# Convolution kernel: two input loads asked for one block earlier

## The chip, the cores and the metric

The kernel runs on one core of a Trainium2 chip. The metric is the device time of one execution in microseconds (us), lower is better. Before the change three runs took 125.30, 125.17 and 125.36 us, median 125.3.

## The reference

The kernel computes a 3 x 3 convolution with padding 1 over 16 images of 64 channels and 64 x 64 pixels, into 128 output channels, all float32 in memory. Nine tenths of the weights are zero, without a pattern that the kernel uses.

```python
batch, c_in, h, w, c_out, k = 16, 64, 64, 64, 128, 3
x_pad = np.pad(x, ((0, 0), (0, 0), (pad, pad), (pad, pad)), mode='constant')
for b in range(batch):
    for co in range(c_out):
        for ci in range(c_in):
            for kh in range(k):
                for kw in range(k):
                    if weight[co, ci, kh, kw] != 0:
                        output[b, co] += weight[co, ci, kh, kw] * x_pad[b, ci, kh:kh+h, kw:kw+w]
```

## The kernel before

**Tiling.** Two images form a pair: 2 x 64 channels fill the 128 partitions. There are eight pairs, 0 to 7, and each is cut into four blocks of 16 output rows, so there are 32 blocks in all, numbered k = 0 to 31; pair p has the blocks 4p to 4p + 3. For a block three inputs are prepared in bfloat16: `sums` (each even row plus the odd row below it), `odd` (the odd rows) and `even` (the even rows). TensorE multiplies them with transformed weights into PSUM, in the order sums, odd, even. One product is shared by the two output rows of a couple; ScalarE copies it from PSUM to `pc`, and VectorE adds it to each of the other two products, writing the even and the odd output rows into a pair's output buffer.

**Who does what.** GpSimd issues all loads of x except the first half of pair 0, and makes `sums` and `even` for the blocks 1 to 31 (lines 287 to 299). ScalarE makes `odd` and `pc` (lines 302 to 307). VectorE does the two additions (lines 310 to 324). SyncE loads the weights and pair 0's first half, and issues the stores (lines 327 to 338, the last one at line 384). TensorE runs a loop of two blocks a turn (lines 368 to 378). Each engine takes its instructions in order, and semaphores tie them together.

**GpSimd's order.** It runs ahead of TensorE by at most two blocks: before it fills `sums` or `even` for block k, it waits until TensorE has finished the product that reads the same buffer for block k - 2. After the fills of block k it issues the load that the table `WHEN` names for k, if there is one:

```python
    PIECES[4] = [(0, 16), (16, H)]
    WHEN = {1: (4, 0), 6: (4, 1), 8: (5, 0), 13: (6, 0)}
...
        for fill_in, product in ((fill_sums, 2), (fill_even, 6)):
            if k >= UNROLL:
                wait(g, s_pe, 6 * (k - UNROLL) + product)
            fill_in(k)
        if k in WHEN:
            load(*WHEN[k])
```

An entry (p, i) is part i of pair p. Pairs 0 (its second half) to 3 are asked for at the start. Pair 4, the fifth, comes in two parts: rows 0 to 15 behind block 1, rows 16 to 63 behind block 6. Pair 5, the sixth, comes whole behind block 8, pair 6 behind block 13, and pair 7 in pieces behind the blocks 18 and 19 (`GROUPS`).

**Loads and buffers.** A load reads float32 from memory and writes bfloat16 into SBUF; only pair 0's first half stays float32. The pairs 0 to 2 lie in the buffer `home`, which becomes an output buffer later; the pairs 3 to 6 have buffers of their own (`x3` to `x6`), so no load of them waits for a buffer. All loads that GpSimd issues go through one DMA queue, q0 in the profile.

**Stores.** SyncE issues the store of pair p once its four blocks are complete: 4 MB a pair, in halves for the pairs 6 and 7. They go through q1. Output buffers are four, taken in turn: `o0`, `o1`, `o2` and `home`; before VectorE writes pair p >= 4 it waits for the store of pair p - 4 (line 315). Loads and stores share the same 16 DMA engines.

Of the kernel before, what the change touches and what calls it, by code (L numbers as in the profile page):

```python
# [22 lines left out]
def kernel(  # L23
# [15 lines left out]
    PIECES = {p: [(0, H)] for p in range(NP)}  # L39
    PIECES[0] = [(HEAD, H)]  # L40
    PIECES[4] = [(0, 16), (16, H)]
    WHEN = {1: (4, 0), 6: (4, 1), 8: (5, 0), 13: (6, 0)}

# [65 lines left out]
    def load(p, i=0):  # L111
        a, b = PIECES[p][i]
        nc.gpsimd.dma_start(out=xs[p][:, a:b, :], in_=pair(p)[:, a:b, :]).then_inc(s_x[p][i], 16)
# [176 lines left out]
    for k in range(1, N):  # L290
# [6 lines that stand above are left out]
        for group in GROUPS.get(k, ()):  # L297
# [124 lines left out]
```

## Time and profile before

| What | us |
|---|---|
| Median of the three runs | 125.30 |
| Profiled execution, its own time | 125.27 |
| Its span, first to last instruction | 123.4 |
| TensorE's first product of block 0 | 7.73 |
| Last addition on VectorE ends | 112.92 |
| Last store issued | 113.21 |
| TensorE busy | 110.1 |
| VectorE busy | 82.6 |
| GpSimd busy | 65.7 |
| ScalarE busy | 54.6 |

The span is the time from the first instruction to the last one. The profiled execution's own time is 1.9 us more than its span, and agrees with the median. Issuing a DMA takes an engine 0.4 to 0.6 us and is not counted as busy time; the transfer itself runs on the 16 DMA engines, and is seen in the rows of the queues: packets, megabytes, and the time of the packets as a share of 16 engines' time in the window. Packets overlap a little, so a full window shows a share slightly over 100%. Bytes are counted where they are written, so that a load from float32 into bfloat16 counts half of what it reads. The issues of the loads and stores that the text speaks of, with the time from issue to landing:

| Transfer | issued at, us | KB written | to landing, us |
|---|---|---|---|
| Pair 4, rows 0 to 15 | 9.31 | 256 | 15.5 |
| Store of pair 0 | 22.17 | 4096 | 16.2 |
| Pair 4, rows 16 to 63 | 24.80 | 768 | 13.8 |
| Pair 5 | 31.28 | 1024 | 16.8 |
| Store of pair 1 | 35.14 | 4096 | 20.2 |
| Pair 6 | 47.49 | 1024 | 15.0 |

### The profile page before, as it was taken

The page shows a single profiled execution, that of the slowest core. Times are in us where ns is not written, and L with a number is a line of the kernel's source. Part 1 is how long each engine was busy: PE and PEld are TensorE (multiplying, and loading weights), DVE is VectorE, ACT ScalarE, POOL GpSimd, SP SyncE. Part 2 cuts the span into 40 slices and gives each one's busy share as a digit, 9 for nine tenths or more (in the row PEclk, how much of TensorE's full clock was granted, in tenths as well). Part 3 has the DMA queues.
Part 4 walks back from the last instruction along what each step waited for, and adds up shares of the span by engine and source line. Part 5 has one row for each costly group of instructions (what it writes and reads, how often), then busy time and mean ns, then how long its engine had stood idle before and what let it go on. Part 6 is the DMA issues. An engine that isn't in the chain of part 4 may idle for free.

```text
span 123.4 us, 2490 instructions
## 1 busy us (share of the span) xinstructions
PE 110.1 (89%) x983; PEld 56.8 (46%) x983; DVE 82.6 (67%) x74; ACT 54.6 (44%) x79; POOL 65.7 (53%) x92
## 2 busy tenths in 40 slices
PE   5999999999999999999999999999999999991000
PEld 1435555555555555555555555555555555550000
DVE  0577777777777777777777777777777777776000
ACT  4544444555555555544444444445555555530000
POOL 4579555575755557555559975555555565200000
PEclk9999999999999999999999999999999999999755
DMA  4999999999999999999999999999999999999993
GB/s 125 350 220 215 215 215 218 274 436 380 324 311 244 321 316 420 388 297 340 345 425 433 357 341 357 408 345 404 424 428 425 425 428 417 428 422 428 428 428 167
DMA packets 4643, 42.79 MB, mean 347 GB/s; under 512 B 538, under 2 KB 538, under 8 KB 1312
## 3 DMA queue, kind: packets, MB, share of 16 engines
q1 hardware_dynamic: 3008, 34.90, 67.5%
q0 software_dynamic: 1632, 7.87, 31.3%
q14 instruction: 3, 0.02, 0.0%
HBM read 17.07 MB, written 33.55 MB: 410 GB/s over the span
## 4 chain that ended last, share of the span: by engine, by line
PE 83%; DVE 2%; issue 0%; DVEq 0%
PE ps L350 83%; DVE home L322 1%; DVE home L318 1%; DVEq L170 0%
## 5 line engine op out<-in xcount | busy, mean ns | idle before, releaser
L305 ACT COPY pc<-ps 128x1024 f32<-128x1024 f32 x32 | 32.4, 1012 | 51.8 <-PE ps L350 51.8
L350 PE MATMUL ps<-even,wT 64*128 64x504 bf16 (+1 forms) x384 | 47.3, 377 | 0.0
L350 PE MATMUL ps<-odd,wT 64*128 64x504 bf16 (+1 forms) x384 | 47.3, 377 | 0.0
L318 DVE TENSOR_TENSOR o<-ps,pc 128x1024 f32<-128x1024 f32 x24 | 29.4, 1225 | 19.6 <-PE ps L350 19.6
L350 PEld LDWEIGHTS ps<-even,wT 64*128 64x128 bf16 x384 | 21.8, 94 | 19.7
L350 PEld LDWEIGHTS ps<-odd,wT 64*128 64x128 bf16 x384 | 21.8, 94 | 19.7
L322 DVE TENSOR_TENSOR o<-ps,pc 128x1024 f32<-128x1024 f32 x24 | 29.4, 1225 | 0.0
L350 PE MATMUL ps<-sums,wT 64*128 64x504 bf16 (+1 forms) x192 | 26.5, 377 | 0.1
L207 POOL TENSOR_TENSOR sums<-x 128x512 bf16<-128x512 bf16 x16 | 18.5, 1156 | 0.1
L196 POOL COPY even<-x 128x576 bf16<-128x576 bf16 (+1 forms) x16 | 10.4, 651 | 14.6 <-PE ps L350 14.6
L350 PEld LDWEIGHTS ps<-sums,wT 64*128 64x128 bf16 x192 | 10.8, 94 | 10.2 <-issue 0.6
L207 POOL TENSOR_TENSOR sums<-home 128x512 bf16<-128x512 bf16 (+1 forms) x11 | 13.3, 1213 | 2.2 <-DMA home<-in_x_dram 2.1
L318 DVE TENSOR_TENSOR home<-ps,pc 128x1024 f32<-128x1024 f32 x8 | 9.8, 1225 | 6.3 <-PE ps L350 6.3
L196 POOL COPY even<-home 128x576 bf16<-128x576 bf16 (+2 forms) x11 | 6.7, 610 | 8.2 <-PE ps L350 8.0
L187 ACT COPY odd<-x 128x576 bf16<-128x576 bf16 (+1 forms) x16 | 10.6, 661 | 0.0
L322 DVE TENSOR_TENSOR home<-ps,pc 128x1024 f32<-128x1024 f32 x8 | 9.8, 1225 | 0.0
L187 ACT COPY odd<-home 128x576 bf16<-128x576 bf16 (+1 forms) x10 | 6.6, 658 | 0.0
L263 PE MATMUL ps<-idle_rhs 128*128 128x512 bf16 x14 | 5.2, 537 | 1.4 <-DVE idle_rhs L228 1.4
L197 POOL MEMSET even<- 128x64 bf16 x8 | 1.2, 154 | 9.4 <-PE ps L350 9.4
L196 POOL COPY even<-x_last 128x576 bf16<-128x576 bf16 (+2 forms) x5 | 2.7, 557 | 4.2 <-PE ps L350 4.2
L207 POOL TENSOR_TENSOR sums<-x_last 128x512 bf16<-128x512 bf16 x4 | 4.6, 1153 | 0.0
L263 PEld LDWEIGHTS ps<-idle_rhs 128*128 128x128 bf16 x14 | 1.7, 130 | 3.7 <-issue 1.9
(26 smaller groups left out, 25.6 us busy)
## 6 DMA issues: line engine op xcount, KB each, us to landing
out_dram<-o SPq DMA_DIRECT2D x5, 4096.0 KB, 19.2
out_dram<-home SPq DMA_DIRECT2D x1, 4096.0 KB, 21.1
out_dram<-o SPq DMA_DIRECT2D x2, 2048.0 KB, 13.6
out_dram<-home SPq DMA_DIRECT2D x2, 2048.0 KB, 10.3
x<-in_x_dram POOLq DMA_DIRECT2D x3, 1024.0 KB, 16.8
home<-in_x_dram POOLq DMA_DIRECT2D x2, 1024.0 KB, 12.8
home<-in_x_dram SPq DMA_DIRECT2D x1, 1024.0 KB, 5.5
x<-in_x_dram POOLq DMA_DIRECT2D x1, 768.0 KB, 13.8
```

The lines of the kernel that those rows point to most:

```text
L187: copy or (lambda o, i: nc.scalar.copy(out=o, in_=i)),
L196: copy or (lambda o, i: nc.gpsimd.tensor_copy(out=o, in_=i)),
L197: zero or (lambda o: nc.gpsimd.memset(o, 0.0)),
L207: engine.tensor_tensor(out=sums[k % UNROLL], in0=src[:, q0 : q0 + ROWS : 2, :], in1=src[:, q0 + 1 : q0 + ROWS : 2, :], op=ADD,).then_inc(s ...
L263: t.matmul(idle_ps, idle_rhs[:, 0:128], idle_rhs, start=True, stop=True)
L305: a.copy(out=pc[k % 3], in_=ps[0]).then_inc(s_pc, 1)
L318: v.tensor_tensor(out=o[:, :, r0 : r0 + ROWS : 2, :], in0=ps[1], in1=pc[k % 3], op=ADD).then_inc(s_free, 1)
L322: v.tensor_tensor(out=o[:, :, r0 + 1 : r0 + ROWS : 2, :], in0=ps[2 + k % 2], in1=pc[k % 3], op=ADD).then_inc(s_out, 1)
L350: mm = t.matmul(into[:, n, :, c_lo:c_hi], tap(g, kw, n), src[q, i : i + HALF, c_lo + kw - 1 : c_hi + kw - 1], start=(m == 0), stop=(m == l ...
```

## The change

One line differs. The second part of pair 4 is asked for behind block 5 in place of block 6, and pair 5 behind block 7 in place of block 8. On GpSimd's queue each of the two load instructions moves up past one `sums` addition and one `even` copy; the other engines' instructions and their order are the same.

```diff
     PIECES[4] = [(0, 16), (16, H)]
-    WHEN = {1: (4, 0), 6: (4, 1), 8: (5, 0), 13: (6, 0)}
+    WHEN = {1: (4, 0), 5: (4, 1), 7: (5, 0), 13: (6, 0)}
```

## The prediction

> **What bounds the kernel now.** I read the page's head and slices first, then the chain of waits, then the DMA queues in chosen windows, and last GpSimd's timeline around the two places. The chain ends with VectorE's last addition (start, length, what):
>
> ```profile
> 7.73 102.64 PE ps L350 x948
> ...
> 111.69 1.23 DVE home L322
> ```
>
> So TensorE runs from 7.73 to 110.37 with nothing between, and the result is complete at 112.92. But the span is 123.4 us, so 10.5 us lie behind the last arithmetic. They belong to the last store, issued at 113.21 (SyncE's timeline):
>
> ```profile
> 113.21 0.37 SPq L384 DMA_DIRECT2D out_dram<-home  x1
> ```
>
> In a window around that issue, time from issue to landing:
>
> ```profile
> out_dram<-home SPq DMA_DIRECT2D x1, 2048.0 KB, 9.4
> ```
>
> 9.4 us for 2.10 MB is too long for the transfer alone. The queue's price comes from a stretch with stores only, 92 to 101 us (queue: packets, MB, share of 16 engines):
>
> ```profile
> q1 hardware_dynamic: 251, 3.88, 101.0%
> ```
>
> 9.0 us for 3.88 MB is 2.32 us per MB, so the last store needs 2.10 x 2.32 = 4.9 us; the other 4.5 us it stood behind earlier stores and the start of a transfer. The slices of the page say since when there is a backlog:
>
> ```profile
> DMA  4999999999999999999999999999999999999993
> GB/s 125 350 220 215 215 215 218 274 436 380 324 311 244 321 316 420 388 297 340 345 425 433 357 341 357 408 345 404 424 428 425 425 428 417 428 422 428 428 428 167
> ```
>
> The 16 DMA engines are full from the second slice to the last but one. Bytes are counted as written; a load reads four bytes for each two it writes, which is why the second to seventh slices show half the rate and are full all the same. Loads only, 8 to 22 us:
>
> ```profile
> q0 software_dynamic: 418, 3.03, 103.7%
> ```
>
> 14.0 us for 3.03 MB is 4.62 us per MB written. With both prices the whole program can be added up: section 3 of the page gives 34.90 MB on q1 and 7.87 MB on q0, so 34.90 x 2.32 + 7.87 x 4.62 = 81.0 + 36.4 = 117.4 us, against about 120 us of busy DMA (from 2 to 122). The kernel is bound by DMA work. What can move its end is the DMA time lost or won, not when a load is asked for.
>
> **The change, GpSimd's side.** No instruction is added or removed. Two load issues move up one block, each past one sums addition and one even copy on GpSimd's queue. GpSimd's timeline of before:
>
> ```profile
> 20.95 0.66 POOL L196 COPY even<-home 128x576 bf16<-128x576 bf16 x1 [1.43 <-PE ps L350]
> 21.62 1.15 POOL L207 TENSOR_TENSOR sums<-home 128x512 bf16<-128x512 bf16 x1
> 24.19 0.66 POOL L196 COPY even<-home 128x576 bf16<-128x576 bf16 x1 [1.43 <-PE ps L350]
> 24.80 0.57 POOL L113 DMA_DIRECT2D x<-in_x_dram  x1
> 25.39 1.16 POOL L207 TENSOR_TENSOR sums<-home 128x512 bf16<-128x512 bf16 x1
> ...
> 28.10 1.16 POOL L207 TENSOR_TENSOR sums<-home 128x512 bf16<-128x512 bf16 x1
> 30.68 0.66 POOL L196 COPY even<-home 128x576 bf16<-128x576 bf16 x1 [1.42 <-PE ps L350]
> 31.28 0.57 POOL L113 DMA_DIRECT2D x<-in_x_dram  x1
> ```
>
> The copy at 20.95 is block 5's even. The first issue goes behind it, to about 21.6. Block 6's sums then run 22.2 to 23.35 in place of 21.6 to 22.8; the copy behind them waits for TensorE until 24.19 anyway, and TensorE takes block 6's sums at 27.17 (its timeline). So 0.57 us is hidden in a wait of 1.43, with 3.8 us left before TensorE would notice. Block 7's sums come 0.54 earlier. The second issue goes from 31.28 to about 28.1; block 8's sums then run 28.7 to 29.8, the copy behind them waits until 30.68, TensorE takes them at 33.66. Cost: 0. If the cover were gone, 2 x 0.57 = 1.1 us of TensorE delay would still lie before the last store's issue at 113.21, which could come some 2.6 us later without emptying the DMA queues (the packets end at about 122.2, so the last store has its turn from 122.2 - 4.9 = 117.3; less about 1.5 us from issue to first byte, as store 0 shows, issued at 22.17 and with no packet in the window to 23.6 and its first in the next). SyncE's queue has the same instructions in the same order.
>
> **The change, who gains from an earlier landing.** Nobody. In the table of waits the only wait for data of x on GpSimd is 2.1 us at the start, on ScalarE 0.4. The second part of pair 4 lands at 24.80 + 13.8 = 38.6 and is first read with block 16, whose even copy needs row 16 at 56.6 (GpSimd's timeline); pair 5 lands at 31.28 + 16.8 = 48.1 and is used from block 20, whose sums come some 19 us later. Worth of 3.2 us earlier: 0.
>
> **The change, the DMA engines.** The loads are 768 and 1024 KB, 0.79 + 1.05 = 1.84 MB, 8.5 us of DMA time at 4.62. Store 0 (issued 22.17) and store 1 (35.14) are 4.19 MB each, 9.7 us. Before, stores ran alone from 24.6 to 28.6 (q1 at 101.4%, no q0), then loads and stores mixed. Now the loads stand behind pair 4's first part, whose last bytes move at about 24.4, and mix with store 0 from its start. Work until 47 is the same either way: store 0 and both loads are done by 24.4 + 9.7 + 8.5 = 42.6, store 1 runs alone behind them. Store 0 lands near 42.6, not 22.17 + 16.2 = 38.4; its buffer is overwritten from block 16, at 61.9 on VectorE, 19 us later. Gain from the order alone: 0, because no engine was empty that now gets work.
>
> One thing is not 0: the price of mixing. Where load 6 mixes with stores, 52 to 61 us, it costs nothing:
>
> ```profile
> q0 software_dynamic: 126, 1.03, 54.6%
> q1 hardware_dynamic: 127, 1.82, 48.3%
> ```
>
> 1.03 x 4.62 + 1.82 x 2.32 = 8.98 us in 9.0. But where the two moved loads run, 28.6 to 42 us:
>
> ```profile
> q1 hardware_dynamic: 188, 2.82, 52.3%
> q0 software_dynamic: 211, 1.34, 50.6%
> ```
>
> 2.82 x 2.32 + 1.34 x 4.62 = 12.73 us in 13.4: **0.67 us of DMA time is lost there**, 0.38 of it from 28.6 to 36.6, 0.23 from 36.6 to 39 and the rest to 42 (same arithmetic). The trace doesn't show why. After the change these loads meet other packets of the stores. Bounds: the loss goes, -0.67; or it spreads over the whole stretch with loads, 24.4 to 42.6, at its worst local rate (0.23 of 2.4, 9.6%): 1.75, so +1.1. At the mean rate of 5% it is 0.91, so +0.24. I take 0, the nearest row being that very stretch with the same loads and the same store.
>
> From 36.6 to 39 q0 has 102.3% and q1 2.8% though store 1 was issued at 35.14: a fresh store starts some 4 us late when a load is under way. The Trainium skill, DMA: Bandwidth & Descriptors, section Queues, rings and completion order, has each engine go round the queues with work after each packet. By that rule the change only swaps turns, and the sum is 0 as well; this row departs from strict turns for 2.4 us, so the rule is no proof that the 0.67 stays.
>
> **Sum.** 0 (GpSimd) + 0 (landings) + 0 (order) + 0 (loss kept, -0.67 to +1.1). The profiled run took 125.27 us (123.4 span and 1.9 around it); the median is 125.30. Forecast 125.3. A measurement of this kernel tells 0.2%, 0.25 us, from no change.
>
> **Rivals.**
> (B) The loss goes, as it is absent where load 6 mixes. For it: of the mixed stretches with large packets this alone loses 5%; the loads now follow one another and end together with store 0, so the start of mixing at 28.6 and the load-only stretch from 36.6 to 39 vanish, where 0.61 of the 0.67 sits or begins. Against: the loss could belong to these addresses, which don't change. Time 125.27 - 0.67 = 124.6 in full, 124.9 for half.
> (C) Slower: the loss grows, because store 0 now shares the engines through its whole length. The place is 24.4 to 42.6 us; the price 5% to 9.6% of 18.2 us against 0.67 now, +0.24 to +1.1, so 125.5 to 126.4, middle 125.8; it decides once the mixed stretch loses over 0.92 us (0.67 + 0.25). For it: the mixing stretch in which a loss is seen gets longer. Against: 52 to 61 mixes as densely at no loss.
> (D) The change does not do what it says at the engines: load bytes don't move earlier, since before there were some 4 us from the issue at 24.80 to first bytes. Then nothing changes, 125.3. Against: here q0 is still working when the request comes, so it follows on.
>
> **From cases to numbers.** Forecast (own range 125.0 to 125.55) 0.34, B 0.32, C 0.30, D 0.04. Range: from nearly all of B (124.5, a little below the full 124.6 for run scatter) to most of C (126.0), leaving out about 0.1 to 0.2. Faster by over 0.2%: B and 0.04 of the forecast's edge, 0.36. Slower: C and 0.03 of the edge, 0.33. Within: 0.31.
>
> **What would show it.** Right: q0 busy without a break from about 24 to 43 in the DMA windows; store 0 landing near 42.6; TensorE's chain still 7.73 to 110.4; the same bytes on both queues; at 52 to 61 us the same rows as before. Which case it is shows in the lost time of 24 to 47 by the two prices: 0.69 us now (1.85 MB and 5.93 MB in 23.0), near 0 for B, over 0.95 for C. Wrong altogether: TensorE idle before block 6 or 8, a different end of the chain, or the last store's 9.4 us changed by something later than 52 us.

## The result and the profile after

The changed kernel is slower. In the first comparison its median is 126.10 us against 125.17 for the kernel before (22 runs each), a ratio of 1.0069 with a 95% interval of 1.0047 to 1.0090. Two later comparisons of the same kernel gave 1.0023 (1.0004 to 1.0042) and 1.0028 (1.0001 to 1.0055). So it costs 0.2 to 0.7%. Medians are those of all executions, ratios and intervals those of the undisturbed ones, so the two can differ slightly. Its profiled execution took 126.35 us with a span of 124.5; before, 125.27 and 123.4.

Arithmetic has not moved. The chain of waits of the changed kernel (start, length, what):

```profile
7.76 102.64 PE ps L350 x948
...
111.73 1.22 DVE home L322
```

TensorE runs the same 102.64 us and VectorE ends at 112.95, before 112.92. On GpSimd the two loads stand where the change puts them:

```profile
20.99 0.66 POOL L196 COPY even<-home 128x576 bf16<-128x576 bf16 x1 [1.42 <-PE ps L350]
21.59 0.57 POOL L113 DMA_DIRECT2D x<-in_x_dram  x1
22.18 1.16 POOL L207 TENSOR_TENSOR sums<-home 128x512 bf16<-128x512 bf16 x1
24.23 0.66 POOL L196 COPY even<-home 128x576 bf16<-128x576 bf16 x1 [0.88 <-PE ps L350]
...
28.11 0.57 POOL L113 DMA_DIRECT2D x<-in_x_dram  x1
```

The wait before block 6's even copy shrinks from 1.43 to 0.88 us, about the 0.57 of the issue, and the copy starts on time. The loss is in the transfers. The slices of the changed kernel:

```profile
DMA  3999999999999999999999999999999999999992
GB/s 121 349 222 216 219 216 213 175 222 338 346 332 321 361 434 437 374 303 308 384 421 397 376 340 390 378 351 433 405 428 426 442 416 416 429 426 424 434 429 95
```

The engines look as full as before. The place shows in the rates: the eighth and ninth slices (21.8 to 28.0 us) move 175 and 222 GB/s, before 274 and 436. The rows of the queues from 23.4 to 28 us (queue: packets, MB, share of 16 engines) in the changed kernel:

```profile
q0 software_dynamic: 157, 0.58, 84.8%
q1 hardware_dynamic: 21, 0.34, 17.8%
```

And in the kernel before:

```profile
q1 hardware_dynamic: 110, 1.80, 91.8%
q0 software_dynamic: 80, 0.13, 15.5%
```

Shares come to over 100% in both. By the prices of the prediction (2.32 us per MB stored, 4.62 per MB loaded) the changed kernel did 0.34 x 2.32 + 0.58 x 4.62 = 3.47 us of work in 4.6 us and lost 1.13; the kernel before lost nothing. A packet that is in flight counts as busy however slowly it goes, so the share alone doesn't show this loss. The bytes do, and so does the time of one packet: from 25 to 26.5 us the changed kernel moves 33 load packets of 6 KB at a share of 98.6%, which is 0.986 x 16 x 1.5 / 33 = 0.72 us each. In the kernel before, from 30 to 33 us, 46 such packets at 45.3% take 0.453 x 16 x 3 / 46 = 0.47 us each. So the loss is packets that take half as long again, not engines that stand empty.

A part of this window shows who moves and who doesn't. From 23.4 to 26.6 us in the changed kernel:

```profile
q0 software_dynamic: 140, 0.48, 105.4%
q1 hardware_dynamic: 3, 0.05, 3.7%
```

Which store stands there? Store 0 was issued at 22.21 and its row says how long it took; the last store's row shows what is left of the loss at the end:

```profile
out_dram<-o SPq DMA_DIRECT2D x1, 4096.0 KB, 23.4
...
out_dram<-home SPq DMA_DIRECT2D x1, 2048.0 KB, 10.4
```

Store 0 lands after 23.4 us in place of 16.2, the last store after 10.4 in place of 9.4. How much of the last store is still to begin at 121.5 us, in the window from there to 126, first in the kernel before:

```profile
q1 hardware_dynamic: 16, 0.04, 2.3%
```

and then in the changed kernel:

```profile
q1 hardware_dynamic: 47, 0.25, 13.5%
```

0.21 MB more, at 2.32 us per MB: the engines are 0.49 us behind on average. From 24 to 47 us (5.75 MB on q1, 1.84 MB on q0) the changed kernel loses 23.0 - 5.75 x 2.32 - 1.84 x 4.62 = 1.16 us, 0.47 more than the 0.69 of before. The loss that the kernel before has from 28.6 to 42 us, 0.67, is gone; the changed kernel's rows there give 13.4 - 3.15 x 2.32 - 1.32 x 4.62 = -0.01 us:

```profile
q1 hardware_dynamic: 192, 3.15, 55.8%
q0 software_dynamic: 190, 1.32, 47.1%
```

The span grew by 1.1. The remainder is put down to unevenness: before, no packet starts after 122.5; in the changed kernel six do, and one of them after 123.0, so some engines end later than the mean. The rows don't tell the 16 engines apart.

### The profile page after: what moved, and what is told of

Read it like the earlier page. It is cut to its first block, busy times and chain, and to the rows that moved or that the text cites. A ratio compares the mean times of both kernels' runs of the same rounds, so it can differ in the third digit from the quotient of the medians.

```text
span 124.5 us, 2490 instructions
## 1 busy us (share of the span) xinstructions
PE 109.9 (88%) x983; PEld 57.3 (46%) x983; DVE 82.6 (66%) x74; ACT 54.6 (44%) x79; POOL 65.7 (53%) x92
## 4 chain that ended last, share of the span: by engine, by line
PE 82%; DVE 2%; issue 0%; DVEq 0%
PE ps L350 82%; DVE home L318 1%; DVE home L322 1%; DVEq L170 0%
## 5 line engine op out<-in xcount | busy, mean ns | idle before, releaser
L350 PE MATMUL ps<-sums,wT 64*128 64x504 bf16 (+1 forms) x192 | 26.5, 377 | 0.4 <-PEq L361 0.4
L207 POOL TENSOR_TENSOR sums<-x 128x512 bf16<-128x512 bf16 x16 | 18.5, 1155 | 0.1
L196 POOL COPY even<-x 128x576 bf16<-128x576 bf16 (+1 forms) x16 | 10.4, 650 | 14.6 <-PE ps L350 14.6
L350 PEld LDWEIGHTS ps<-sums,wT 64*128 64x128 bf16 x192 | 10.9, 94 | 10.4 <-issue 0.8
## 6 DMA issues: line engine op xcount, KB each, us to landing
out_dram<-home SPq DMA_DIRECT2D x1, 4096.0 KB, 23.4
x<-in_x_dram POOLq DMA_DIRECT2D x1, 768.0 KB, 13.4
```

Of the source, the lines that this page charges most:

```text
L196: copy or (lambda o, i: nc.gpsimd.tensor_copy(out=o, in_=i)),
L207: engine.tensor_tensor(out=sums[k % UNROLL], in0=src[:, q0 : q0 + ROWS : 2, :], in1=src[:, q0 + 1 : q0 + ROWS : 2, :], op=ADD,).then_inc(s ...
L350: mm = t.matmul(into[:, n, :, c_lo:c_hi], tap(g, kw, n), src[q, i : i + HALF, c_lo + kw - 1 : c_hi + kw - 1], start=(m == 0), stop=(m == l ...
```

## The experiments

Below, "lost from 16 to 62 us" is 46 us less the work done in them by the two prices. The window takes in all that the versions move; packets over its edges make it uncertain by one or two tenths. It is 1.11 us for the kernel before and 1.50 for the change.

**e1: only the second part of pair 4 moves.**

```diff
-    WHEN = {1: (4, 0), 6: (4, 1), 8: (5, 0), 13: (6, 0)}
+    WHEN = {1: (4, 0), 5: (4, 1), 8: (5, 0), 13: (6, 0)}
```

> Only the second part of pair 4 moves (behind block 5); pair 5 stays behind block 8. In the profile of the changed kernel the DMA engines lose most of their extra time from 23.4 to 26.6 us, where that part moves alone right behind the first part and store 0, issued at 22.2, has not begun: 0.48 MB x 4.62 + 0.05 MB x 2.32 = 2.35 us of work in 3.2. Theory (that part's early request is the cost): slower than before by 0.5 to 1.0 us, about the same as the full change, and the same loss of some 0.85 us between 23.4 and 26.6. Rival (pair 5 behind it, so that store 0 shares the engines through its whole length): no change, within 0.25 us.

Measured: 125.85 us against 125.50, ratio 1.0015 (0.9992 to 1.0038). The theory's 0.5 to 1.0 us is missed: 0.15% is 0.2 us, which the rival allows, and the time alone leaves the question open. Its rows from 23.4 to 28 us don't:

```profile
q0 software_dynamic: 174, 0.68, 101.6%
q1 hardware_dynamic: 4, 0.07, 3.4%
```

0.68 x 4.62 + 0.07 x 2.32 = 3.30 us of work in 4.6: 1.30 lost, as with the full change, with pair 5 still behind block 8. From 16 to 62 us it loses 1.96. The profiled execution took 126.22, above its own median, so these sizes are those of a run worse than the usual one. In it the store was issued at 23.07 and the load 0.62 us ahead, as in the change.

**e2: only pair 5 moves.**

```diff
-    WHEN = {1: (4, 0), 6: (4, 1), 8: (5, 0), 13: (6, 0)}
+    WHEN = {1: (4, 0), 6: (4, 1), 7: (5, 0), 13: (6, 0)}
```

> Only pair 5 moves (behind block 7); the second part of pair 4 stays behind block 6. Theory (the cost is the other request): within 0.25 us of before, and the window 23.4 to 26.6 with stores at over 90% as before. Rival (pair 5 is the cost): slower by 0.5 to 1.0 us.

Measured: 125.48 against 125.50, ratio 0.9991 (0.9968 to 1.0014). Lost from 16 to 62 us: 1.04; nothing from 23.4 to 28. Pair 5's request is free, and the loss hangs on pair 4's second part. It also repeats the kernel before's own loss: 0.64 us from 28.6 to 42, before 0.67.

**e3: the second part a block earlier still.**

```diff
-    WHEN = {1: (4, 0), 5: (4, 1), 7: (5, 0), 13: (6, 0)}
+    WHEN = {1: (4, 0), 4: (4, 1), 7: (5, 0), 13: (6, 0)}
```

> The second part of pair 4 is asked for behind block 4 (about 18.4 us), a block earlier still, with pair 5 behind block 7. Its packets still move from about 24 us, but its request is then 5 us old and not under 2. If the loss comes from a request that is too fresh when its turn comes, it goes: within 0.3 us of before. If it comes from that part's packets meeting the start of store 0 (issued at 22.2 in both), it stays: slower by 0.5 to 1.0 us, with some 0.85 us lost from 23.4 to 26.6.

Measured: 126.26 against 125.50, ratio 1.0042 (1.0020 to 1.0065). A request that is 5 us old costs as well, so its freshness isn't the cause. The profiled execution took 127.64, far above the median, and its rows are not read.

**e4: pair 4 in one load.**

```diff
-    PIECES[4] = [(0, 16), (16, H)]
-    WHEN = {1: (4, 0), 5: (4, 1), 7: (5, 0), 13: (6, 0)}
+    PIECES[4] = [(0, H)]
+    WHEN = {1: (4, 0), 7: (5, 0), 13: (6, 0)}
```

> Pair 4 is asked for in one load behind block 1, and pair 5 behind block 7. Same bytes; rows of 64 x 64 in one piece, and no packets of 2 KB and 6 KB written. If any load that moves alone while store 0 starts loses time, this is slower than before by 0.5 to 1.0 us with the loss again between 23.4 and 27 us. If the loss belongs to the cut in two (two loads over the same rows of memory, packets of 6 KB), it is within 0.3 us of before or faster.

Measured: 125.50 against 125.50, ratio 0.9996 (0.9977 to 1.0016). By its time this speaks for the cut as the cause, by its profile against: from 23.4 to 28 us it loses 4.6 - 0.66 x 4.62 - 0.33 x 2.32 = 0.79 us with no cut and no packets of 6 KB. It saves something elsewhere: the small packets of the first part are dear. In the kernel before, from 22.2 to 23.6, q0 wrote 0.25 MB in 1.4 us, 0.24 us more than the price of large ones. From 16 to 62 us the lost time is 1.32 against 1.11; those 0.2 us are within its interval. So the loss in the rows doesn't need the cut; that it costs time without the cut isn't shown.

**e5 and e9: the change, measured twice more.**

> The changed kernel once more, beside the others of this group on one chip. Theory so far: a store that is freshly issued while loads keep the DMA engines busy makes the load packets in front of it slow until its own first packets move; the change lets pair 4's second part run on exactly when store 0 is issued (22.2 us), where the kernel before had only the last packets of the small first part. Expected: slower by 0.3 to 0.9%, with 0.8 to 1.4 us lost from 23.4 to 28 us and the last packets of the span 0.5 us or more apart from the first engine's last. A rival would be that the 0.7% belongs to one chip: then within 0.2%.

> The changed kernel a third time, since its two intervals so far are 1.0047 to 1.0090 and 1.0004 to 1.0042 times the kernel before. Theory: between 0.2 and 0.7% slower, with about 1 us lost between 23.4 and 28 us. Rival (chance on one chip): within 0.2%.

Measured: 125.94 against 125.57, ratio 1.0023 (1.0004 to 1.0042), and 125.90 against 125.56, ratio 1.0028 (1.0001 to 1.0055). Lost from 23.4 to 28 us: 0.90 and 0.88. The loss is there each time and smaller than the 1.13 of the first profile. The 0.23% of e5 lies below its expected 0.3 to 0.9%; e9 lies within its own. The unevenness is smaller too: in neither does a packet start after 123.0.

**e6: store 0 in two halves, loads as before.** The first half is then issued at 15.88, beside loads of whole pairs that nobody moved.

```diff
-    HALVED = (6, 7)
+    HALVED = (0, 6, 7)
...
-            wait(v, s_st[p - 4][0], 16)
+            for landed in s_st[p - 4]:
+                wait(v, landed, 16)
```

> The table of loads as before; pair 0's store goes out in two halves, so that the first is issued behind block 1, at about 15.7 us, beside loads of whole pairs. Theory (a fresh store beside running loads): 0.5 us or more lost in 16 to 21 us, where the kernel before loses nothing (loads alone, 4.62 us per MB); the time is slower by 0.2 to 0.8 us unless losses at 28.6 to 42 go. Rival (the loss belongs to pair 4's or pair 5's rows in memory): nothing lost in 16 to 21 us, within 0.25 us of before.

Measured: 125.57 against 125.57, ratio 0.9996 (0.9979 to 1.0014). The rows from 16 to 22 us:

```profile
q0 software_dynamic: 143, 1.04, 90.4%
q1 hardware_dynamic: 32, 0.26, 10.7%
```

And in the kernel before, where loads run alone in this window:

```profile
q0 software_dynamic: 175, 1.30, 103.9%
```

1.04 x 4.62 + 0.26 x 2.32 = 5.41 us of work in 6.0: 0.59 lost, before -0.01. With the store's issue 6.3 us earlier, a loss appears among loads of other pairs and other addresses. No byte of store 0 moves before 19.4 us, 3.5 us after its issue; most of the loss, 0.38, lies from 18.5 to 20.5 us, around the store's start. Another 0.57 us is lost from 23.4 to 28, where the kernel before loses nothing. In exchange the loss from 28.6 to 42 falls from 0.67 to 0.12 and that from 42 to 62 from 0.33 to 0.05. The total from 16 to 62 is 1.20 against 1.11, which fits a time that stands still.

**e7 and e11: the request just behind store 0's issue.** GpSimd asks for pair 4's second part between block 6's sums and its even copy; pair 5 stays behind block 7, as in the change.

```diff
-    WHEN = {1: (4, 0), 5: (4, 1), 7: (5, 0), 13: (6, 0)}
+    WHEN = {1: (4, 0), 7: (5, 0), 13: (6, 0)}
+    BETWEEN = {6: (4, 1)}
...
             fill_in(k)
+            if product == 2 and k in BETWEEN:
+                load(*BETWEEN[k])
```

> The second part of pair 4 is asked for between block 6's sums and its even copy, about 22.8 us: a little after store 0's issue at 22.2, where the change asks at 21.6 and the kernel before at 24.8; pair 5 behind block 7 as in the change. Theory (what counts is whether large loads stand in front of store 0 when it is issued): as before within 0.25 us, stores moving at 87% or more from 23.4 to 26.6. Rival (any request that comes this early costs): slower by 0.5 to 1.0 us.

> The version with pair 4's second part between block 6's sums and even copy and pair 5 behind block 7, again. Expected: 0.2 to 0.6% faster than the kernel before; no loss from 23.4 to 26.6 us. If the first measurement was chance: within 0.2%.

Measured: 125.09 against 125.57, ratio 0.9963 (0.9942 to 0.9985), and 125.12 against 125.56, ratio 0.9955 (0.9926 to 0.9984). This beats both kernels, which the first expectation didn't foresee. In its profile the issue comes at 23.16, 0.54 us behind store 0's at 22.62. The rows from 23.4 to 28 us:

```profile
q1 hardware_dynamic: 108, 1.77, 96.5%
q0 software_dynamic: 81, 0.13, 15.8%
```

The store has the engines, as in the kernel before, and nothing is lost. The change asks 0.62 us ahead of the store's issue (21.59 and 22.21), this version 0.54 us behind it; nothing else differs in the program between 0.2 to 0.7% slower and 0.4% faster. The loss from 28.6 to 42 falls to 0.30 and 0.34; from 16 to 62 it is 1.01 in the first profile, whose execution of 125.51 us was 0.4 above its median, and 0.76 in the second.

**e8: pair 5 late.**

```diff
-    WHEN = {1: (4, 0), 6: (4, 1), 8: (5, 0), 13: (6, 0)}
+    WHEN = {1: (4, 0), 6: (4, 1), 11: (5, 0), 13: (6, 0)}
```

> Pair 5 is asked for behind block 11 (about 41 us) in place of block 8; all else as before. Store 1 is issued at 35.1 with only the end of pair 4's second part beside it. Theory: the loss from 36.6 to 39, where pair 5 runs alone while store 1 starts, goes (0.23 us by the kernel before's rows, 0.3 with its neighbours), and some 0.15 us comes where pair 5 begins beside a running store; so 0 to 0.3 us faster. Rival (the losses at 36 to 41 belong to pair 5's rows): they move with pair 5 to 45 to 50 us, no change.

Measured: 125.49 against 125.57, ratio 0.9995 (0.9977 to 1.0013). The loss from 28.6 to 42 falls from 0.67 to 0.47, as expected in direction. The rival's place, 42 to 50, loses nothing (-0.06). But from 42 to 62 it loses 0.69, where the kernel before loses 0.33: store 2, issued at about 48.4, now meets the loads of pairs 5 and 6 running alone, and moves nothing from 50 to 52. Neither side had expected that. The loss went to the next fresh store, and the time, within the expected 0 to 0.3 us, doesn't tell the two sides apart.

**e10 and e12: pair 5's place with the request between.** Against the version of e7, pair 5 goes behind block 8, and behind block 6:

```diff
-    WHEN = {1: (4, 0), 7: (5, 0), 13: (6, 0)}
+    WHEN = {1: (4, 0), 8: (5, 0), 13: (6, 0)}
...
-    WHEN = {1: (4, 0), 7: (5, 0), 13: (6, 0)}
+    WHEN = {1: (4, 0), 6: (5, 0), 13: (6, 0)}
```

> Pair 4's second part between block 6's sums and even copy (about 22.8 us, just behind store 0's issue), pair 5 behind block 8 as before the change. If the gain of the version with pair 5 behind block 7 comes from this request alone, this one is 0.2 to 0.5% faster than before too. If pair 5's place matters with it (loads must follow one another so that none begins anew beside a store), it lies between, within 0.2%.

> As the version before it, but pair 5 asked for behind block 6, right after pair 4's second part. The queue of the loads is then never empty before 44 us either way, so within 0.15% of that version, and 0.2 to 0.6% faster than the kernel before. If a load's early request costs by itself, it is slower than that version by 0.3% or more.

Measured, against 125.56: 125.23, ratio 0.9968 (0.9936 to 1.0001), and 125.07, ratio 0.9965 (0.9939 to 0.9991). With e11 at 0.9955 on the same chip the three can't be told apart: pair 5's place is free here too, although the interval of e10 just reaches 1. Lost from 16 to 62 us: 0.69 and 0.53.

Over these versions, e3 left out, the profiled execution follows the time lost from 16 to 62 us: 0.53 to 0.76 lost goes with 124.90 to 125.35 us (e10 to e12), 1.01 to 1.20 with 125.27 to 125.70 (before, e2, e6, e7, e8), and 1.32 to 1.96 with 125.72 to 126.35 (e1, e4, e5, e9 and the first profile of the change).

## Why the prediction was wrong

**GpSimd: right.** No copy was delayed, TensorE's chain has the same length, and the waits took up the 0.57 us.

**Landings: right that nobody gains.** Nothing waits for these loads, before or after.

**The DMA bound: right.** Arithmetic and bytes stayed the same, and the end followed the DMA time that was lost.

**The order of transfers: here the prediction failed.** It said that the loads "mix with store 0 from its start", that the sum of the order alone is 0, and took the loss as kept. They don't mix from its start: store 0 has 3 packets from 23.4 to 26.6 us, and the loads run alone in front of it. The prediction had the row that says so, a fresh store "starts some 4 us late when a load is under way", for store 1 at 36.6 to 39, where it had also counted 0.23 us lost in 2.4. It used that row to doubt a rule and didn't carry it to store 0, which the change puts in the same position. The price of that position, 1.13 us from 23.4 to 28, stood at 0 in the sum. The prediction's own sign shows it too: store 0 was to land near 42.6 and lands at 22.21 + 23.4 = 45.6.

**The loss: the bounds held, the value taken did not.** From 24 to 47 us it went from 0.69 to 1.16, +0.47 where 0 was taken: about the new 1.13, less the 0.68 that vanished from 28.6 to 42.

**What had no term:** that the engines can be held up unequally, so that the span ends with the worst of them. This is argued from the last packets and not shown engine by engine. Of the 1.1 us in the profiled spans, about half is the mean (0.49) and the remainder is put down to this.

**Rival B was half right.** The loss from 28.6 to 42 did vanish, from 0.67 to -0.01; a larger one arose ahead of it.

**Rival C had the sign, and not the mechanism.** Its 125.5 to 126.4 us hold the measured time, but by luck. It let the loss spread over the mixed stretch to 42.6; the mixed stretch loses nothing, and the loss sits before the mixing begins. Its point of decision, over 0.92 us lost in the whole stretch, was passed with 1.16; e5 and e9, at 1.07 and 0.97, passed it too, and are slower by about 0.3 us. **D is out:** load bytes moved earlier.

The Trainium skill's rule in DMA: Bandwidth & Descriptors, section Queues, rings and completion order, that each engine goes round its queues after each packet, fits the mixed stretches, as far as equal numbers of packets show it (192 and 190 in the change from 28.6 to 42 us); from 23.4 to 26.6 us, with 140 and 3, the trace doesn't show turns.

**Shown:** the loss comes where a store is issued into running loads (e6 brings one about by moving the store, e7 removes it by asking just behind the issue), and neither a fresh request nor pair 5 is needed (e3, e1). The loss in the rows doesn't need the cut either (e4). **Not shown:** that the time grows without the cut (e4's didn't), why load packets are slow around the start of a fresh store, why the first comparison showed 0.7% and the later two 0.2 to 0.3%, and what sets which engine is hit.

## What to carry to other kernels

In a kernel whose DMA engines are full, asking for data earlier than anyone needs it is not always free: look at what the other queue issues at that moment, and try to let the store go first and the load just behind it. Look for where the loss goes, too: e6 and e8 only moved it. Count bytes against time in windows, or work out the time of one packet, since busy shares stay near 100% while packets crawl. And the end can come later than the mean of the 16 engines tells.

## What was not expected of the hardware

A store issued while large loads fill the engines starts 3.5 to 4.5 us later (issued at 22.21, three packets by 26.6; in e6 issued at 15.88, none by 19.4; in e1 issued at 23.07, none by 27.5), and issued when the loads are running out it starts after about 1.5 us (in the kernel before, issued at 22.17, with packets from 23.6). Around its start the loads themselves slow down: 0.6 to 1.3 us of 16 engines' time a store (0.59 in e6, 0.88 to 1.13 in the change, 1.30 in e1). Once both queues run, large packets can mix at no cost that these rows can tell (-0.01 us from 28.6 to 42 in the change). A load that begins beside running stores also starts late (in the kernel before, asked for at 24.80, with no packet by 29.5) and has a smaller price of the same kind: in e7, from 27 to 30 us, 3.0 - 0.72 x 2.32 - 0.16 x 4.62 = 0.59 us, and 0.38 from 28.6 to 36.6 in the kernel before.
